# Router logits from un-normalised rows, a five-bit search for two experts, weight tiles split ahead of the first gather

## The chip, the cores and the metric

One NeuronCore of a Trainium2 chip. The time is the device time of one execution, in microseconds (us); lower is better. The kernel before: median 2549.72 us of 3 runs (2549.34 to 2553.43). Engines are named as in the profile: PE (matrix products), ACT, DVE, POOL, SP (issues transfers). Each is a queue that runs its instructions in order.

## The reference

Two layers over 1024 latent rows and 256 context rows of 1024 features. Each layer mixes the rows (Fourier heads, pooling groups, attention), projects them out, and then sends them through 16 experts, of which each takes the 128 latent rows (32 context rows) that like it best:

```python
x_new = x + g1 * ox                                   # x_mid
h = modulate(x_new, norm2_g[i], sh2, sc2)             # rms norm * g * (1 + scale) + shift
logits = jnp.einsum('bnd,de->bne', h, w_router)
aff = jax.nn.softmax(logits, axis=-1)
g, idx = lax.top_k(aff.transpose(0, 2, 1), cap)       # cap = 2 n / 16
xs = jax.vmap(lambda hb, ib: hb[ib])(h, idx)
a, u = xs @ w_gate, xs @ w_up
y = (silu(a) * u) @ w_down * g                        # scattered back and added
```

The second layer has no experts over context rows. All in float32.

## The kernel before, in words

Every value that enters a product is split into two parts (`split`, line 247: ACT copies the high part, DVE subtracts to get the low part), and each product is made of three: 6 matmuls of 128x512 for a weight tile of 128x1024. Tiles live in 43 pages of 128x1024 (`pg`), halves (`hf`) and quarters (`qt`), with 8 PSUM banks. All instructions go through one helper, so that the profile puts them all on line 107; they are told apart by tile names. A scheduler orders the instructions of each engine when the kernel is built; what sets the order is the dependences, the order in which the code emits work, and manual dependences (`tc.add_manual_dep`).

`out_proj` (line 991) goes over the row tiles (eight of the latent rows): `project(t)` (999) multiplies, adds to the residual (x_mid, `mid`), squares on ACT, takes the inverse root on POOL, and on DVE makes the modulated norm in two passes, which goes to a table in DRAM (`table`). `route(t)` (1031), one tile later, transposes the normed tile by 8 PE transposes (through `cs`, the identity), copies it on ACT (`hf`), multiplies by the router's weights in four column groups, copies (`qt`), transposes, and reduces to 16 logits per row. After the last tile come the softmax and the affinities (`aff`).

`Choice` (1081) finds, per expert, the threshold that leaves just 128 rows: `search(which)` (1107) builds the bits of the threshold three at a time in ten rounds, 7 candidates an expert. A round is: compare all affinities with all candidates (DVE), count with a product by ones (PE, 8 matmuls), keep the candidates that hold (DVE), take the maximum (DVE), set the next candidates (DVE). `finish` (1138) turns the thresholds into places. The latent rows have three groups: experts 0 to 3, 4 to 9, 10 to 15. `pick` (1174) makes a one-hot of an expert's places (DVE), multiplies it by the rows' numbers and gates (PE), and gives an index; `gather` (1211) fetches the 128 rows by an indirect transfer that POOL issues.

`Experts` (1232): `fetch` (pick and gather), `enter` (transposes and splits the gathered rows), `product` (1262: a weight tile a step: split it, 6 matmuls), `middle`, `leave` (scales and scatters to `out_dram`, by POOL), `ahead` (prefetches weight tiles into free pages). In layer 1 the first search runs alone (line 1567); then the 24 product steps of each expert (gate, up, down) run interleaved with the other two searches, a search step every two product steps. The gathers of experts 2 and 3 come right after expert 0's up product, since both belong to the first group. In layer 0 expert 0's gate and up run beside both searches of the context rows, then 8 steps of the second latent search run alone, and the rest goes beside the gate products of experts 1 to 7, seven steps each.

## Time and profile before

| | |
|---|---|
| median of 3 runs | 2549.72 us (2549.34 to 2553.43) |
| span of the profiled execution | 2549.8 us |
| PE busy | 2425.8 us, 95% |
| DVE busy | 1934.4 us, 76% |
| ACT busy | 1383.9 us, 54% |
| POOL busy | 327.6 us, 13% |
| transfers | 575.51 MB, 226 GB/s over the span |

No other time of the profiled execution than its span is given. The profile shows one execution. Its page gives busy times and 40 slices of the span; windows give the same for chosen stretches, with the granted clock of PE (1.00 is 2.4 GHz); the timeline gives single instructions, with the idle time before one and what ended it.

### The profile page before, as it was taken

The page shows a single profiled execution, that of the slowest core. Times are in us where ns is not written, and L with a number is a line of the kernel's source. Part 1 is how long each engine was busy: PE and PEld are TensorE (multiplying, and loading weights), DVE is VectorE, ACT ScalarE, POOL GpSimd, SP SyncE. Part 2 cuts the span into 40 slices and gives each one's busy share as a digit, 9 for nine tenths or more (in the row PEclk, how much of TensorE's full clock was granted, in tenths as well). Part 3 has the DMA queues.
Part 4 walks back from the last instruction along what each step waited for, and adds up shares of the span by engine and source line. Part 5 has one row for each costly group of instructions (what it writes and reads, how often), then busy time and mean ns, then how long its engine had stood idle before and what let it go on. Part 6 is the DMA issues. An engine that isn't in the chain of part 4 may idle for free. (4 is left out here: it accounts for less than half of the span.)

```text
span 2549.8 us, 39656 instructions
## 1 busy us (share of the span) xinstructions
PE 2425.8 (95%) x14709; PEld 1841.9 (72%) x14709; DVE 1934.4 (76%) x3114; ACT 1383.9 (54%) x1934; POOL 327.6 (13%) x350
## 2 busy tenths in 40 slices
PE   7999899999899999999999889899995999999998
PEld 3878667775677777777777567688774777888886
DVE  4537757756988787777777685877746999999997
ACT  4124546422555656666666412466523777787775
POOL 1321000001111011121010252100000111001100
PEclk9999999999999999999999999999996999999999
DMA  7103341547798899899897661100566999999993
GB/s 287 51 24 119 108 133 36 182 147 263 269 287 295 279 285 300 288 290 303 284 294 241 218 215 50 40 1 1 198 224 221 352 344 366 385 381 386 384 397 98
DMA packets 175074, 575.51 MB, mean 226 GB/s; under 512 B 22360, under 2 KB 35064, under 8 KB 174880
## 3 DMA queue, kind: packets, MB, share of 16 engines
q1 hardware_dynamic: 162784, 535.22, 59.1%
q0 software_dynamic: 12096, 37.75, 6.2%
q8 instruction: 115, 1.88, 0.3%
q14 instruction: 79, 0.65, 0.1%
HBM read 535.10 MB, written 37.80 MB: 225 GB/s over the span
## 5 line engine op out<-in xcount | busy, mean ns | idle before, releaser
L107 PE MATMUL banks<-pg,pg 128*128 128x512 f32 (+2 forms) x9656 | 1987.1, 393 | 10.5 <-DVE pg L107 7.8
L107 PEld LDWEIGHTS banks<-pg,pg 128*128 128x128 f32 (+1 forms) x9656 | 1451.7, 172 | 389.3 <-issue 30.2
L107 ACT ACTIVATE pg<-pg 128x1024 fp32r<-128x1024 f32 (+3 forms) x945 | 932.3, 1008 | 529.4 <-PE banks L107 348.2
L107 DVE TENSOR_TENSOR pg<-pg,pg 128x1024 fp32r<-128x1024 f32 (+3 forms) x918 | 1040.2, 1158 | 195.2 <-ACT pg L107 180.7
L107 ACT ACTIVATE pg<-banks 128x512 fp32r<-128x512 f32 (+3 forms) x438 | 243.6, 581 | 281.4 <-PE banks L107 271.6
L107 DVE TENSOR_TENSOR pg<-banks,pg 128x512 fp32r<-128x512 f32 (+2 forms) x404 | 257.4, 663 | 79.2 <-ACT pg L107 73.9
L107 PE MATMUL banks<-cs,pg 128*128 128x128 f32 x1616 | 239.3, 279 | 38.7 <-DVE pg L107 28.9
L107 PEld LDWEIGHTS banks<-cs,pg 128*128 128x128 f32 x1616 | 191.9, 142 | 93.8 <-DVE pg L107 44.2
L107 ACT ACTIVATE hf<-banks 128x512 f32<-128x512 f32 (+3 forms) x126 | 66.3, 541 | 241.5 <-PE banks L107 225.3
L107 PE MATMUL banks<-pg,hf 128*128 128x512 f32 (+1 forms) x660 | 162.7, 366 | 11.9 <-ACT pg L107 7.6
L107 PEld LDWEIGHTS banks<-pg,hf 128*128 128x128 f32 x660 | 113.2, 194 | 44.1 <-ACT pg L107 10.5
L107 DVE TENSOR_REDUCE mx<-banks 128x1 f32<-128x256 f32 (+1 forms) x136 | 106.6, 795 | 31.5 <-PE banks L107 30.5
L107 ACT ACTIVATE pg<-banks,nb 128x256 f32<-128x256 f32 (+1 forms) x136 | 104.0, 773 | 40.2 <-DVE nb L107 35.3
L107 POOL TENSOR_SCALAR rnv<-ss 128x1 f32<-128x1 f32 x38 | 17.1, 451 | 670.1 <-ACT pg L107 600.2
L107 POOL DMA_INDIRECT pg<-xtab,idxx x32 | 44.8, 1401 | 424.5 <-PE banks L107 165.9
L107 POOL DMA_INDIRECT xmid<-pg,idxx x16 | 37.3, 2329 | 446.9 <-DVE pg L107 446.9
L107 DVE TENSOR_TENSOR hf<-banks,pg 128x512 f32<-128x512 f32 x36 | 24.8, 689 | 65.6 <-PE banks L107 65.5
L107 POOL DMA_INDIRECT out_dram<-pg,idxx x16 | 36.3, 2271 | 244.6 <-DVE pg L107 116.6
L107 PE MATMUL banks<-pg,qt 128*32 128x256 f32 x1024 | 60.1, 388 | 0.5 <-ACT qt L107 0.5
L107 PE MATMUL banks<-pg,cond 128*32 128x512 f32 x256 | 56.6, 617 | 2.1 <-DMA pg<-in_ada_w_dram 2.1
L107 DVE TENSOR_TENSOR pg<-pg,hf 128x512 f32<-128x512 f32 (+1 forms) x68 | 42.5, 626 | 20.1 <-POOL hf L107 19.1
L107 PEld LDWEIGHTS banks<-pg,qt 128*32 128x32 f32 x1024 | 32.1, 112 | 26.6 <-issue 4.5
(148 smaller groups left out, 1082.9 us busy)
## 6 DMA issues: line engine op xcount, KB each, us to landing
pg<-in_w_gate_dram SPq DMA_DIRECT2D x256, 512.0 KB
pg<-in_w_up_dram SPq DMA_DIRECT2D x256, 512.0 KB
pg<-in_w_down_dram SPq DMA_DIRECT2D x256, 512.0 KB
pg<-in_ada_w_dram SPq DMA_DIRECT2D x96, 512.0 KB
pg<-in_w_in_dram SPq DMA_DIRECT2D x32, 512.0 KB
pg<-in_x_dram SPq DMA_DIRECT2D x16, 512.0 KB
pg<-in_w_out_dram SPq DMA_DIRECT2D x16, 512.0 KB
xtab<-pg SPq DMA_DIRECT2D x16, 512.0 KB
```

The costliest lines, as they stand in the source:

```text
L107: r = fn(*a, **k)
```

## The change

1. *Router.* `route` transposes x_mid instead of the normed tile. The router's weights are multiplied once by g (1 + scale) of their feature, and a bias (shift times weights) is made by eight matmuls; each tile's logits then take one more DVE operation, logit * r + bias. The norm itself moves behind the square for all tiles but the last, and behind the last logits for the last one.
2. *Search.* Four groups of latent experts: 0 and 1, 2 to 5, 6 to 10, 11 to 15. The first is searched five bits at a time: six rounds of 31 candidates an expert.
3. *Places.* Expert 1's one-hot may not come ahead of expert 0's index on DVE.
4. *Split ahead.* `begin(4)`: four weight tiles of expert 0 are split ahead of the products, in layer 1.
5. *Order of layer 1.* The second search (experts 2 to 5) runs beside the first 26 product steps, the gather of expert 2 comes at step 5 of expert 0's down product, that of expert 3 with expert 1's up product; the other two searches follow at a step every two product steps. Eight pages more are left free ahead of the first search (`spare + 8`).
6. *Order of layer 0.* Beside expert 0's products run one search of the context rows and the second latent one; the eight steps that ran alone are gone; the other three searches go beside experts 1 to 7, nine steps each.

The core of the diff:

```diff
@@ out_rows
+        SP.dma_start(cb[0:8, 0:128], part(4))
+        SP.dma_start(cb[8:16, 0:128], part(3))
+        SP.dma_start(cb[16:24, 0:128], norm2_g[i].rearrange("(k p) -> k p", p=128))
+        ps = bank()
+        PE.transpose(ps[:, 0:24], cb[0:24, 0:128], ident[:24, :24])
+        col = sm("rcol", [128, 24])
+        DVE.tensor_copy(col, ps[:, 0:24])
...
+        for k in range(KT):
+            PE.matmul(ps[:, 0:16], col[:, 8 + k:9 + k].to_broadcast([128, 128]), wr[:, k, 0:16],
+                      start=(k == 0), stop=(k == KT - 1))
+        base = sm("rbase", [128, 16])
+        DVE.tensor_copy(base, ps[:, 0:16])
...
+        DVE.tensor_tensor(out=wr, in0=wr, in1=col[:, 0:8, None].to_broadcast([128, 8, 32]), op=OP.mult)
@@ project
-            r = rsq("rn", ss, 1, D)
-            for cols in [slice(512 * n, 512 * n + 512) for n in range(2)] if t == st.nt - 1 else [slice(0, 1024)]:
-                DVE.scalar_tensor_tensor(h[:, cols], xt[:, cols], r, a2[:, cols], op0=OP.mult, op1=OP.mult)
-                DVE.tensor_add(h[:, cols], h[:, cols], b2[:, cols])
-            drop(xt)
-            SP.dma_start(table[rws, :], h.ap)
-            held[t] = h
+            held[t] = xt, h, rsq("rn", ss, 1, D)
+            if t < st.nt - 1:
+                normed(t)
+
+        def normed(t):
+            xt, h, r = held[t]
+            DVE.scalar_tensor_tensor(h.ap, xt.ap, r, a2.ap, op0=OP.mult, op1=OP.mult)
+            DVE.tensor_add(h.ap, h.ap, b2.ap)
+            SP.dma_start(table[128 * t:128 * t + 128, :], h.ap)
+            drop(h)
@@ route
-            h = held.pop(t)
+            h, _, r = held[t]
...
+            DVE.scalar_tensor_tensor(logit[:, t, :], logit[:, t, :], r, base, op0=OP.mult, op1=OP.add)
+            if t == st.nt - 1:
+                normed(t)
@@ Choice
-            self.groups = ((0, 4), (4, 6), (10, 6)) if st.nt == 8 else ((0, 8), (8, 8))
+            self.groups = ((0, 2), (2, 4), (6, 5), (11, 5)) if st.nt == 8 else ((0, 8), (8, 8))
...
-            for it in range(10):
+            J, rounds, j0 = (32, 6, 80) if n == 2 else (8, 10, 0)
+            m = J - 1
...
+            for it in range(rounds):
@@ pick
+            if e == 1:
+                tc.add_manual_dep(one.ins, picked[nm], order, reason="the first expert's place first")
@@ Experts
+        def begin(self, n):
+
+            for k in range(n):
+                raw = self.came.pop((0, "g", k))
+                wp = self.ready[0, "g", k] = Pair(page)
+                split(wp(0, 1024), raw.ap)
+                drop(raw)
@@ layers
-            ex.ahead(pre[1], spare)
+            ex.ahead(pre[1], spare + 8)
             run(cho.search(0))
...
             ex.fetch(0)
+            ex.begin(4)
             ex.fetch(1)
...
-            rest = chain(cho.search(1), cho.search(2))
+            rest = chain(cho.search(2), cch.search(1), cho.search(3))
...
-                    side = [(some(rest, 7), 7)] if e < 8 else []
+                    side = [(some(rest, 9), 9)] if e < 8 else []
...
-                    interleave((chain(ex.gate(e, True), ex.up(e, True)), 16), (cch.search(0), 20), (cch.search(1), 20))
+                    interleave((chain(ex.gate(e, True), ex.up(e, True)), 16), (cch.search(0), 20), (cho.search(1), 20))
...
-                    run(some(rest, 8))
...
-                        if 1 < e and e + 2 < NE:
+                        if e and e + 2 < NE:
                             ex.fetch(e + 2)
...
-                        if e == 0:
-                            ex.fetch(2)
-                            ex.fetch(3)
...
-                        yield from ex.down(e, False)
+                        yield from at(ex.down(e, False), {} if e else {5: lambda: ex.fetch(2)})
                         ex.leave(e)
-            interleave((products(), 24 * NE), (later(rest, 4), 12 * NE))
+            work = products()
+            interleave((some(work, 26), 26), (later(cho.search(1), 3), 24))
+            interleave((work, 24 * NE - 26), (rest, 12 * NE - 16))
```

What it does to the order of the instructions is seen at three places. First, DVE at the last row tile of layer 1, before (`hf<-banks` is half of the output projection times its gate, `pg_17221` x_mid, `pg_17278` the norm, `lmxx` the softmax's maximum):

```order
L107 TENSOR_TENSOR hf_17274<-banks,pg_16520 128x512
L107 TENSOR_TENSOR pg_17221<-pg_17221,hf_17274 128x512
L107 COPY qt_17307<-banks 128x128
L107 TENSOR_REDUCE logitx_3898<-banks 128x16
L107 SCALAR_TENSOR_TENSOR pg_17278<-pg_17221,rnr_100,pg_16522 128x512 x2
L107 TENSOR_TENSOR pg_17278<-pg_17278,pg_16527 128x512 x2
L107 COPY qt_17331<-banks 128x128
L107 TENSOR_REDUCE logitx_3898<-banks 128x16
L107 TENSOR_REDUCE lmxx_4838<-logitx_3898 128x8
```

And DVE there now (`pg_17401` is x_mid, `pg_17458` the norm; `pg_17712`, `pg_17716` and `pg_17780` are low parts of weight tiles):

```order
L109 TENSOR_TENSOR hf_17454<-banks,pg_16677 128x512
L109 TENSOR_TENSOR pg_17712<-pg_17067,pg_17711 128x1024
L109 TENSOR_TENSOR pg_17401<-pg_17401,hf_17454 128x512
L109 COPY qt_17482<-banks 128x128
L109 TENSOR_TENSOR pg_17716<-pg_17069,pg_17715 128x1024
L109 TENSOR_REDUCE logitx_3919<-banks 128x16
L109 TENSOR_TENSOR pg_17780<-pg_17071,pg_17779 128x1024
L109 SCALAR_TENSOR_TENSOR logitx_3919<-logitx_3919,rnr_101,rbase_3912 128x16
L109 COPY qt_17507<-banks 128x128
L109 SCALAR_TENSOR_TENSOR pg_17458<-pg_17401,rnr_100,pg_16679 128x1024
L109 TENSOR_REDUCE logitx_3919<-banks 128x16
L109 TENSOR_TENSOR pg_17458<-pg_17458,pg_16684 128x1024
```

Three splits of weight tiles now stand among the operations of the last tile, the first of them ahead of the last addition to x_mid, and the norm's two passes stand on either side of the last reduction.

Second, POOL's transfers at the start of the experts of layer 1, before (gathers of experts 0, 1, 2, 3 and the first scatter):

```order
L107 DMA pg_17589<-xtab_16532,idxx_5203 128x1024
L107 DMA pg_17605<-xtab_16532,idxx_5204 128x1024
L107 DMA pg_17844<-xtab_16532,idxx_5205 128x1024
L107 DMA pg_17860<-xtab_16532,idxx_5202 128x1024
L107 DMA out_dram<-pg_18125,idxx_5203 1024x1024
```

And now:

```order
L109 DMA pg_17701<-xtab_16706,idxx_5156 128x1024
L109 DMA pg_17733<-xtab_16706,idxx_5157 128x1024
L109 DMA out_dram<-pg_18341,idxx_5156 1024x1024
L109 DMA pg_18312<-xtab_16706,idxx_5158 128x1024
L109 DMA pg_18358<-xtab_16706,idxx_5155 128x1024
```

The gathers of experts 2 and 3 (`idxx_5158`, `idxx_5155`) have moved behind the scatter of expert 0.

Third, PE now at the place where expert 2's rows (`pg_18312`) are transposed; the products with `hf_18344` make expert 3's index, and those of expert 2's index stand right ahead of them; `hf_18327` is a compare of the third search:

```order
L109 MATMUL banks<-auxx_4890,hf_18344 128x5
L109 LDWEIGHTS ones_b
L109 MATMUL banks<-hf_18327,ones_b 128x35
...
L109 MATMUL banks<-pg_18460,pg_17937 128x512 x2
L109 MATMUL banks<-pg_18471,pg_17937 128x512 x2
L109 MATMUL banks<-pg_18471,pg_17938 128x512 x2
L109 MATMUL banks<-pg_18472,pg_17937 128x512 x2
L109 MATMUL banks<-pg_18486,pg_17937 128x512
L109 MATMUL banks<-cs,pg_18312 128x128 x8
```

The transposes stand nine matmuls of 128x512 behind a round of the search and the products that make the index; before, more than a hundred matmuls stood between.

## Rows read from the trace of the kernel before

**Rows 1.** The page: busy time, share and instructions of PE; its granted clock in 40 slices.

```profile
PE 2425.8 (95%) x14709; PEld 1841.9 (72%) x14709; DVE 1934.4 (76%) x3114; ACT 1383.9 (54%) x1934; POOL 327.6 (13%) x350
...
PEclk9999999999999999999999999999996999999999
```

**Rows 2.** Windows, layer 1: length; busy PE, PEld, DVE, ACT, POOL; PEclk; DMA; GB/s.

```profile
1920.00:1940.00 20.00, 6.63 (x89) 4.49 (x90) 11.44 (x43) 1.50 (x3) 2.77 (x5) 0.50 1.00 387
1940.00:1960.00 20.00, 7.90 (x82) 6.00 (x81) 11.11 (x35) 2.94 (x4) 2.50 (x2) 0.51 0.44 160
2040.00:2060.00 20.00, 19.37 (x114) 14.94 (x113) 19.52 (x34) 13.39 (x15) 3.33 (x2) 1.00 0.95 320
2300.00:2320.00 20.00, 20.00 (x104) 16.31 (x103) 18.59 (x20) 17.88 (x21) 3.29 (x2) 1.00 1.01 363
```

**Rows 3.** Timeline, layer 1's last tile: start, us, engine, operation, out<-in, [idle <-releaser].

```profile
1915.63 0.69 DVE L107 TENSOR_TENSOR pg<-pg,hf 128x512 f32<-128x512 f32 x1
...
1918.57 1.41 DVE L107 SCALAR_TENSOR_TENSOR pg<-pg,rnr,pg 128x512 f32<-128x512 f32 x2 [0.60 <-POOL rnr L107]
1919.90 1.29 DVE L107 TENSOR_TENSOR pg<-pg,pg 128x512 f32<-128x512 f32 x2
...
1920.74 1.94 PE L107 MATMUL banks<-cs,pg 128*128 128x128 f32 x8 [3.02 <-DVE pg L107]
...
1924.08 0.29 DVE L107 COPY qt<-banks 128x128 f32<-128x128 f32 x1 [2.89 <-PE banks L107]
...
1925.19 0.29 DVE L107 TENSOR_REDUCE lmxx<-logitx 128x8 f32<-128x128 f32 x1
```

**Rows 4.** Timeline, first search of layer 1: first compare, first product, start of the finish.

```profile
1927.07 0.39 DVE L107 TENSOR_TENSOR hf<-affx,cand 128x224 bf16<-128x224 f32 x1
...
1927.51 0.37 PE L107 MATMUL banks<-hf,ones_b 128*128 128x28 bf16 x8 [2.61 <-DVE hf L107]
...
1942.43 0.34 DVE L107 TENSOR_TENSOR hf<-affx,sel 128x32 bf16<-128x32 f32 x2
```

**Rows 5.** Timeline, places of expert 0, index, gather.

```profile
1945.06 2.36 DVE L107 TENSOR_TENSOR hf<-s1x,cs 128x1024 bf16<-128x1024 f32 x2
...
1946.34 0.38 PE L107 MATMUL banks<-auxx,hf 128*128 128x5 bf16 x8 [2.86 <-DVE hf L107]
...
1948.54 0.15 DVE L107 SCALAR_TENSOR_TENSOR idxx<-pkx 128x1 int32<-128x1 f32 x1
...
1949.49 1.55 POOL L107 DMA_INDIRECT pg<-xtab,idxx  x1 [19.33 <-DVE pkx L107]
```

**Rows 6.** Timeline, experts 0 and 1 of layer 1, DVE and PE.

```profile
1963.10 11.45 DVE L107 TENSOR_TENSOR pg<-pg,pg 128x1024 fp32r<-128x1024 f32 x10
...
1987.37 0.50 DVE L107 TENSOR_TENSOR hf<-affx,cand 128x336 bf16<-128x336 f32 x1
...
1988.53 0.37 PE L107 MATMUL banks<-hf,ones_b 128*128 128x42 bf16 x8
1988.75 3.59 PE L107 MATMUL banks<-pg,pg 128*128 128x512 f32 x14
```

**Rows 7.** All waits of PE from 1956 to 2130: total us, times, longest.

```profile
PE banks L107 <- DVE pg L107: 3.3, 5, 0.8
```

**Rows 8.** Timeline of POOL, scatters of experts 0 and 1 in layer 1.

```profile
2009.42 4.01 POOL L107 DMA_INDIRECT out_dram<-pg,idxx  x1 [22.43 <-DVE cand L107]
2047.75 1.56 POOL L107 DMA_INDIRECT out_dram<-pg,idxx  x1 [34.32 <-DVE pkx L107]
```

**Rows 9.** DMA issues at 1945, 1980 and 2085: gathers, times, median us to landing.

```profile
pg<-xtab,idxx POOLq DMA_INDIRECT x2, 5.0
...
pg<-xtab,idxx POOLq DMA_INDIRECT x2, 9.4
...
pg<-xtab,idxx POOLq DMA_INDIRECT x1, 11.3
```

**Rows 10.** Window of layer 0, expert 0. Columns as in rows 2.

```profile
660.00:680.00 20.00, 14.52 (x94) 10.46 (x93) 17.93 (x64) 6.32 (x8) 2.03 (x2) 0.83 0.59 190
```

77 lines of the change are left out of this document (46 added, 31 removed).

## The prediction

> **What bounds the kernel now.** I read the page first, then the windows, the timeline around the one thin place, the waits and the DMA issues. On the page [rows 1] PE is busy 2425.8 of 2549.8 us, and its clock row holds one slice of 40 that falls to 6. The windows [rows 2] show what that slice is: from 1920 to 1940 PE is busy 6.63 of 20 us at a granted clock of 0.50 (the lower level, 1.2 GHz), between the output projection of layer 1 and its first expert. Everything there is one chain: the last tile's router logits [rows 3], ten search rounds for experts 0 to 3 [rows 4], the places of expert 0, its gather, and its transposes [rows 5]. Work taken off that chain is time, one for one. After it the expert stage of layer 1 is held by two engines at once: 19.37 us of PE and 19.52 us of DVE in 20 while searches run beside the products, 20.00 and 18.59 when they are over [rows 2]. So an added search round costs there at least its slot on PE, and DVE has little room.
>
> The profiled execution (2549.8 us) is 0.1 us above the median of the runs, so the sum applies to either.
>
> **The chain to the first gather.** Router: the last transposes start at 1920.74, after both halves of the norm; x_mid is there at 1915.63 + 0.69 = 1916.32 [rows 3]. From x_mid itself they could start 4.4 us sooner. But in the new DVE order one split of a weight tile (1.14 us, ten in 11.45 [rows 6]) stands ahead of the last x_mid add, so 3.3 us sooner, at 1917.5. The copy of the logits came 3.34 us after the transposes (1924.08), so now at 1920.8. Behind it stand the norm's two passes, 1.41 + 1.29 us [rows 3], ahead of the last logits: 1920.8 + 0.29 + 1.41 + 0.23 + 1.29 + 0.2 = 1924.2 for the maximum, against 1925.19. I take **-1.0 us**; ends 0 (another split comes late) and -3.3 (the norm slips behind).
>
> Search: ten rounds took 15.36 us, from 1927.07 to 1942.43 [rows 4], less 0.50 for a compare of another search among them: 1.49 a round. A new round compares 496 elements instead of 224. The rows give 0.39 us for 224 and 0.50 for 336 [rows 4, 6], 0.001 us an element, so 0.66. The product with ones over 62 columns instead of 28 isn't shown: at least the 0.37 us of the 28 columns [rows 4], at most 0.82 (by columns). Three small operations grow by about 0.03 each. So 1.85 to 2.3 us, and I take 2.0, nearer the low end, since the eight products of 28 and of 42 columns both read 0.37 [rows 4, 6]. Six rounds are 12.0, and one compare of another search (0.39) stays among them: **-3.0 us** (-1.2 to -3.9).
>
> Places: two one-hots of 2.36 us stood ahead of the first index, which came at 1948.54; one is enough, since the product with it starts at 1946.34, 1.28 us in [rows 5]. With 0.38 for the product, a copy and the index after it, the index is there at about 1947.0: **-1.5 us**. Together the first gather starts 5.5 us sooner.
>
> **The expert stage of layer 1.** It now holds 30 rounds and three finishes instead of 20 and two. A round's slot on PE is 1988.75 - 1988.53 = 0.22 us [rows 6]; a finish has a few more and smaller products, which I put at three slots, 0.6. So +2.2 + 0.6 = **+2.8 us** on PE. On DVE the added work is larger, about 0.7 us a round, 7 us in all. Against it stand five weight tiles split before the gather lands and a sixth during it, 1.14 each, 6.8 us. PE waited for DVE 3.3 us in this stage [rows 7], and DVE can regain that when PE is held up (next paragraph). I take **-3.0**; ends 0 and -3.3. Splitting ahead gains nothing more at the first products, as far as I can see, since PE runs them at 0.51 of its clock until about 1960 [rows 2].
>
> The new wait: the gather of expert 2. Before, the gathers of experts 2 and 3 were issued together near 1984 [rows 9], and the only waits that PE has in this stage are on DVE [rows 7]. Now its index follows the second search, and the order of PE has its transposes only two eights of small products, one round and nine matmuls behind the products that make the index. After those products DVE still does the other one-hot (1.22 us), a copy, a compare and the index, some 2.2 us. From index to gather issue took 0.8 us (1948.54 + 0.15 to 1949.49 [rows 5]). Landing took 5.0 us with an idle memory system, 9.4 and 11.3 with weights streaming [rows 9]. At the new place weights stream (DMA share 0.95 in the window at 2040 [rows 2]), so I take 9.4: 12.4 us from the products on. PE has in the same time 1.3 us to the other one-hot's end, its products, the round, and nine matmuls of 0.24 us, 4.6 us in all. The stall is **+7.8 us**; ends 3.4 (a landing in 5.0) and 9.7 (in 11.3). What is queued behind: every product of PE; DVE comes three tiles further and then waits for expert 1's up product, which PE has behind the transposes. That is where the 3.0 us above is regained. POOL has the scatter of expert 0 ahead of this gather; it should be issued by then.
>
> The Trainium skill (DMA: Bandwidth & Descriptors, "Anatomy of one DMA — SWDGE (gpsimd) path") fits one such transfer as 2.0 us plus its bytes over 436 GB/s; for 512 KB an estimate from that page is 3.2 us. By that rule the stall would be 1.6 us and the sum 6.2 us lower. The rows above differ from it even where nothing else moves.
>
> **The rest.** The bias of the router is made three times by a transpose and eight matmuls of 16 columns, plus three small loads. No row shows these; the nearest, eight products of 28 columns, is 0.37 us, the other end 1.94 (eight transposes at the lower clock [rows 3]). I take 0.4 each, **+1.2** (0 to 5). The fused multiply-add per tile's logits (0.2 us) and the longer table of bits cost nothing: they lie beside PE's products in the output projection, where DVE's last halves waited for PE; without that cover they would be 0.2 us for each of 18 tiles. Two weight tiles fewer are fetched ahead of the search; PE's waits show none on weights [rows 7], so nothing.
>
> Layer 0: its expert 0 runs one search of the context and one of the latent rows beside its products, and four rounds that stood alone behind it go. PE is busy 14.52 us of 20 between 660 and 680 [rows 10], 5.5 idle. I take 3.0 of it back (0 to 5.5). Ten more rounds and a finish beside later products, where PE is full, cost 2.8. So **-0.2** (-4 to +4).
>
> **Sum.** -1.0 - 3.0 - 1.5 + 2.8 - 3.0 + 7.8 + 1.2 - 0.2 = +3.1 us: 2552.8 us. The measurement tells 0.2% (5.1 us) from no change, so this is no change.
>
> **Rivals.**
> 1. *The gather of expert 2 lands quickly.* For it: 5.0 us at the first gather, and the page's rule. Against: 9.4 at the same stage with the same stream. The stall is 3.4, the sum -1.3, 2548.4 us; with the rule's 3.2 us it would be 2546.6.
> 2. *Slower: the gather waits behind the scatter of expert 0 on POOL.* The scatters take 1.56 to 4.01 us to issue [rows 8], and the one ahead of the gather was the 4.01. If it starts less than 4 us ahead of the index, the gather starts up to 4 us later, and the stall is 11.8: 2556.8 us. Decided where the stall passes 9.8 us, since all else sums to -4.7. Against: expert 0's down product ends some 8 us of PE ahead of the index's products.
> 3. *The chain hardly shortens:* splits and norm ahead of the logits eat the router's gain, and a five-bit round takes 2.3 us. -2.7 instead of -5.5: 2555.6 us.
> 4. *Faster: everything that hides work does.* Norm behind the logits (-3.3), layer 0 at -4, the stall at 3.4: 2549.8 - 3.3 - 3.0 - 1.5 + 2.8 - 3.3 + 3.4 + 1.2 - 4 = 2542.1 us.
>
> **How the numbers follow.** The forecast has 0.43, rival 1 0.25, rival 2 0.14, rival 3 0.07, rival 4 0.11. Faster by over 0.2% (below 2544.6) takes rival 4 and some of rival 1 where layer 0 gains too: 0.26. Slower (above 2554.8) takes rivals 2 and 3 and the upper edge of the forecast: 0.30. The range reaches from near rival 4 to the forecast with a stall of 9.7 and layer 0 at +4, 2543 to 2560.
>
> **What would show it.** Right: first gather about 5.5 us earlier; six rounds near 2.0 us; a wait of PE on the gather of expert 2 near 2030 of some 8 us; almost no wait of PE on DVE around it. Wrong: no such wait, or rounds over 2.4 us, or a scatter that ends just ahead of that gather.

## The result, and the profile after

The changed kernel takes 2568.85 us (median of 4 runs, 2568.56 to 2570.76) against 2549.53 for the kernel before on the same chip (4 runs): a ratio of 1.0074, interval 1.0062 to 1.0087. It is slower by 19 us. The forecast was 2552.8 with a range up to 2560; the result lies outside.

The page after, busy time and granted clock:

```profile
span 2566.8 us, 40140 instructions
PE 2439.2 (95%) x14902; PEld 1852.2 (72%) x14902; DVE 1946.4 (76%) x3208; ACT 1384.0 (54%) x1934; POOL 333.1 (13%) x350
...
PEclk9999999999899999999999999999997999999999
```

Beside [rows 1] PE is busy 13.4 us longer. The slice of layer 1 that read 6 in the clock row reads 7, and a second one below 9 has come up: the eleventh, at some 640 to 705 us, in layer 0.

**Where the time went.** The products of the weight tiles (`banks<-pg,pg`, 128x512) come 9656 times in both kernels. I took the start of the n-th of them in each trace, counted from 0, and subtracted the one of before. A step from one column to the next is time lost or won between those two products:

```
product       1000  1600  1800  2000  3300  3700  6900  7000  7300  7400  7600  last
changed       -1.6   0.4   5.0   6.5   6.8   9.9  12.1  14.4  14.3   9.4  17.4  17.4
```

Product 1000 to 1600 is the end of attention and the output projections of layer 0, 1600 to 2000 its expert 0, 3300 to 3700 its experts 6 and 7, 6900 to 7000 the start of the output projection of layer 1, 7300 to 7400 the chain to the first gather of layer 1, and 7400 to 7600 the two experts behind it. So the chain wins 4.9 us, the stage behind it loses 8.0, and 14.3 have been lost before the chain starts. Such a row is one execution. e14 below runs the changed kernel again: its steps differ from these by up to 1.3 us, and the one from 7400 to 7600 by 3.4 (11.3 instead of 8.0).

**The chain to the first gather of layer 1** went nearly as the prediction had it. Timeline after, DVE's own (start, us, engine, line, operation, out<-in, [idle before <-releaser]):

```profile
1929.60 0.69 DVE L109 TENSOR_TENSOR hf<-banks,pg 128x512 f32<-128x512 f32 x1
1930.20 1.22 DVE L109 TENSOR_TENSOR pg<-pg,pg 128x1024 fp32r<-128x1024 f32 x1
1931.33 0.69 DVE L109 TENSOR_TENSOR pg<-pg,hf 128x512 f32<-128x512 f32 x1
...
1935.33 1.28 DVE L109 SCALAR_TENSOR_TENSOR pg<-pg,rnr,pg 128x1024 f32<-128x1024 f32 x1 [0.21 <-POOL rnr L109]
...
1938.06 0.29 DVE L109 TENSOR_REDUCE lmxx<-logitx 128x8 f32<-128x128 f32 x1
...
1939.93 0.67 DVE L109 TENSOR_TENSOR hf<-affx,cand 128x496 bf16<-128x496 f32 x1
...
1952.49 0.26 DVE L109 TENSOR_TENSOR hf<-affx,sel 128x16 bf16<-128x16 f32 x2
...
1954.96 1.23 DVE L109 TENSOR_TENSOR hf<-s1x,cs 128x1024 bf16<-128x1024 f32 x1
...
1956.86 0.16 DVE L109 SCALAR_TENSOR_TENSOR idxx<-pkx 128x1 int32<-128x1 f32 x1
```

And PE's and POOL's:

```profile
1940.66 0.57 PE L109 MATMUL banks<-hf,ones_b 128*128 128x62 bf16 x8 [5.01 <-DVE hf L109]
1942.77 0.57 PE L109 MATMUL banks<-hf,ones_b 128*128 128x62 bf16 x8 [1.53 <-DVE hf L109]
...
1957.82 1.36 POOL L109 DMA_INDIRECT pg<-xtab,idxx  x1 [14.17 <-DVE pkx L109]
...
1962.37 1.97 PE L109 MATMUL banks<-cs,pg 128*128 128x128 f32 x8 [3.71 <-DMA pg<-xtab,idxx]
```

Before, the last half started here:

```profile
1914.90 0.69 DVE L107 TENSOR_TENSOR hf<-banks,pg 128x512 f32<-128x512 f32 x1 [4.12 <-PE banks L107]
```

The split of a weight tile stands ahead of the last x_mid add, one pass of the norm ahead of the last logits, as foretold. From the last half of the projection to the maximum of the logits it is 1938.06 - 1929.60 = 8.46 us; before, from 1914.90 to the maximum at 1925.19 [rows 3], 10.29 us. A round takes 2.11 us (1942.77 - 1940.66), the compare 0.67. First compare to finish: 12.56 us against 15.36 [rows 4]. One-hot to index: 1.90 against 3.48 [rows 5]. Last half to gather: 28.22 against 34.59, so 6.4 us gained.

**Behind it,** PE at the transposes of expert 2:

```profile
2026.74 0.35 PE L109 MATMUL banks<-auxx,hf 128*128 128x5 bf16 x8
...
2029.22 3.91 PE L109 MATMUL banks<-pg,pg 128*128 128x512 f32 x9 [1.12 <-DVE pg L109]
2033.96 1.09 PE L109 MATMUL banks<-cs,pg 128*128 128x128 f32 x8 [0.83 <-DMA pg<-xtab,idxx]
...
2043.12 3.27 PE L109 MATMUL banks<-pg,pg 128*128 128x512 f32 x13 [0.86 <-DVE pg L109]
```

POOL there, then the transfers issued from 2027 to 2034 (median us to landing):

```profile
2020.26 2.51 POOL L109 DMA_INDIRECT out_dram<-pg,idxx  x1 [59.49 <-DVE cand L109]
2028.50 1.53 POOL L109 DMA_INDIRECT pg<-xtab,idxx  x1 [5.73 <-DVE pkx L109]
```

```profile
pg<-xtab,idxx POOLq DMA_INDIRECT x2, 5.8
```

The gather is issued 1.76 us after the products (the scatter is long out of the way) and lands in 5.8 us (the median of the two), not 9.4. PE waits for it 0.83 us, not 7.8. It waits for DVE before and behind, and the nine matmuls between take 3.91 us, where the prediction had 0.24 for each: in the window from 2028 to 2034 the granted clock is 0.72.

```profile
2020.00:2028.00 8.00, 7.71 (x61) 5.96 (x59) 8.00 (x25) 5.10 (x6) 2.51 (x1) 1.00 0.99 289
2028.00:2034.00 6.00, 4.04 (x14) 2.62 (x10) 5.54 (x12) 3.17 (x3) 2.65 (x2) 0.72 0.84 273
```

(Length; busy PE, PEld, DVE, ACT, POOL; clock; DMA; GB/s.) DVE has no idle time in the eight us ahead of the stop: in this execution it is DVE that is late, not the gather.

The second execution of the same kernel (e14) shows the same stop and another wait:

```profile
2026.60 2.45 PE L109 MATMUL banks<-pg,pg 128*128 128x512 f32 x9 [1.12 <-DVE pg L109]
2033.41 1.97 PE L109 MATMUL banks<-cs,pg 128*128 128x128 f32 x8 [4.37 <-DMA pg<-xtab,idxx]
```

Here the nine matmuls take 2.45 us, the two gathers land in 7.7 us (median), and PE waits 4.37 us for the first of them. Seven traces have this order of layer 1 (changed, e1, e3, e4, e6, e13, e14). PE waits for the gather 0.45 to 1.09 us in five of them, 2.74 in e4 and 4.37 in e14; from product 7400 to 7600 the five lose 7.7 to 8.2 us, e4 10.9 and e14 11.3. So most of the loss comes without the gather, and a late landing adds to it.

Where the changed kernel's 8.0 us go: PE stands 3.0 us longer (2.2 for DVE, 0.8 for the gather), the 200 weight products take 2.3 longer, the search's products 1.5, and transposes and index products that lie in the stretch the rest.

**Layer 0, expert 0.** Windows after, same columns:

```profile
640.00:660.00 20.00, 19.90 (x119) 15.22 (x118) 19.82 (x49) 12.59 (x14) 0.00 (x0) 1.00 0.98 389
660.00:680.00 20.00, 10.84 (x109) 8.16 (x109) 17.83 (x84) 3.24 (x4) 1.04 (x1) 0.66 0.27 79
680.00:700.00 20.00, 16.92 (x165) 10.68 (x164) 11.33 (x13) 9.52 (x11) 3.91 (x1) 0.83 0.71 226
```

PE is busy 10.84 us of the 20 where it had been 14.52 [rows 10]. The timeline of PE shows why:

```profile
667.20 0.25 PE L109 MATMUL banks<-hf,ones_b 128*128 128x56 bf16 x2 [1.57 <-DVE hf L109]
...
668.81 0.25 PE L109 MATMUL banks<-hf,ones_b 128*128 128x56 bf16 x2 [0.71 <-DVE hf L109]
...
685.82 1.94 PE L109 MATMUL banks<-cs,pg 128*128 128x128 f32 x8 [3.08 <-DMA pg<-ctab,idxc]
```

The products of expert 0 are over at 660, and rounds of both searches (56 columns the context's, 28 the latent rows') are left over. They run alone, a pair in 1.61 us (668.81 - 667.20), until 672. Why so many are left is in DVE's order. Its timeline beside the products, after:

```profile
647.01 0.27 DVE L109 TENSOR_TENSOR hf<-affc,cand 128x112 bf16<-128x112 f32 x1
647.20 0.38 DVE L109 TENSOR_TENSOR hf<-affx,cand 128x224 bf16<-128x224 f32 x1
647.50 1.22 DVE L109 TENSOR_TENSOR pg<-pg,pg 128x1024 fp32r<-128x1024 f32 x1
...
649.10 1.22 DVE L109 TENSOR_TENSOR pg<-pg,pg 128x1024 fp32r<-128x1024 f32 x1
...
650.46 1.22 DVE L109 TENSOR_TENSOR pg<-pg,pg 128x1024 fp32r<-128x1024 f32 x1
651.60 0.27 DVE L109 TENSOR_TENSOR hf<-affc,cand 128x112 bf16<-128x112 f32 x1
```

And before, at the same place:

```profile
644.86 0.45 DVE L107 TENSOR_TENSOR hf<-affc,cand 128x112 bf16<-128x112 f32 x2
645.24 1.22 DVE L107 TENSOR_TENSOR pg<-pg,pg 128x1024 fp32r<-128x1024 f32 x1
...
647.13 0.46 DVE L107 TENSOR_TENSOR hf<-affc,cand 128x112 bf16<-128x112 f32 x2
```

Before, a pair of rounds has one split of a weight tile in it and takes 2.3 us (647.13 - 644.86). After, it has three and takes 4.6 (651.60 - 647.01). The splits hurry on: product 1744, at the end of expert 0's gate and up products, starts at 657.5 against 661.1 before. PE gains 3.6 us there, and then waits for the rounds that stayed behind: product 1752, the first of what follows, starts at 675.1 against 670.0. The context's places and its gather come behind the rounds too (POOL issues it at 678.74; before, at 670.01), and PE waits 3.08 us for its landing, 1.57 before (2.53 in e14).

What PE waited for in that window before isn't what the prediction took it for:

```profile
667.18 0.19 PE L107 MATMUL banks<-auxc,hf 128*128 128x5 bf16 x1 [1.28 <-DVE hf L107]
...
674.24 0.37 PE L107 MATMUL banks<-hf,ones_b 128*128 128x42 bf16 x8
...
677.42 0.63 PE L107 MATMUL banks<-cs,pg 128*128 128x128 f32 x4 [1.57 <-DMA pg<-ctab,idxc]
```

Of the 5.5 us idle between 660 and 680 [rows 10], 3.9 are waits for DVE, for splits and one-hots above all, and 1.57 the wait for the context's gather. The four rounds that the code runs alone start at 674.24, 679.51, 683.50 and 686.63, with other products between them, and PE has no idle time ahead of any. Taking them away had none of this idle time to give back.

**The bias of the router,** PE in layer 1:

```profile
1809.84 1.86 PE L109 MATMUL banks<-qt,rcol 128*128 128x16 f32 x16
```

The eight products are 16 entries in the trace, and take 1.86 us of PE at the full clock (1.00 from 1800 to 1820), in a stretch where PE is busy 19.94 of 20 us. The prediction had 0.4 for each of the three sets.

### The profile page after: what moved, and what is told of

The parts are those of the page before. It is cut to its first block, busy times and chain, and to the rows that moved or that the text cites. A ratio compares the mean times of both kernels' runs of the same rounds, so it can differ in the third digit from the quotient of the medians.

```text
span 2566.8 us, 40140 instructions
## 1 busy us (share of the span) xinstructions
PE 2439.2 (95%) x14902; PEld 1852.2 (72%) x14902; DVE 1946.4 (76%) x3208; ACT 1384.0 (54%) x1934; POOL 333.1 (13%) x350
## 5 line engine op out<-in xcount | busy, mean ns | idle before, releaser
L109 DVE TENSOR_TENSOR pg<-pg,pg 128x1024 fp32r<-128x1024 f32 (+2 forms) x915 | 1041.5, 1161 | 204.1 <-ACT pg L109 185.3
L109 PEld LDWEIGHTS banks<-pg,hf 128*128 128x128 f32 x660 | 112.6, 194 | 45.2 <-ACT pg L109 10.9
L109 PEld LDWEIGHTS <-ones_b 128*128 128x128 bf16 x800 | 29.5, 99 | 48.2 <-issue 47.8
L109 PE MATMUL banks<-hf,ones_b 128*128 128x35 bf16 (+11 forms) x800 | 39.4, 182 | 23.4 <-DVE hf L109 22.6
```

The costliest lines, as they stand in the source:

```text
L109: r = fn(*a, **k)
```

## The experiments

Each ran beside the kernel before on its chip; a ratio is to that, with its interval. In the text, "changed" is the kernel after. Executions of one kernel spread by some 5 us to either side of the median (once by 11), so differences below about 2 us are left alone unless many runs stand behind them. A trace is one execution: those of e1, e3, e5, e8 and e15 lie 2.5 to 4.6 us below their medians, those of e2, e6 and e9 2.9 to 3.8 above, so that a time read from traces and one from medians need not agree. None leaves out part of the outputs' computation; the one that computes something beyond them says so.

### e1: layer 0 as it was

```diff
 class Choice:
-    self.groups = ((0, 2), (2, 4), (6, 5), (11, 5)) if st.nt == 8 else ((0, 8), (8, 8))
+    new = ((0, 4), (4, 6), (10, 6)) if old else ((0, 2), (2, 4), (6, 5), (11, 5))
...
-            rest = chain(cho.search(2), cch.search(1), cho.search(3))
+            rest = chain(cho.search(1), cho.search(2))
...
-                    side = [(some(rest, 9), 9)] if e < 8 else []
+                    side = [(some(rest, 7), 7)] if e < 8 else []
...
-                    interleave(..., (cch.search(0), 20), (cho.search(1), 20))
+                    interleave(..., (cch.search(0), 20), (cch.search(1), 20))
...
+                    run(some(rest, 8))
```

> The changed kernel with layer 0 as it was: the latent groups 0-3, 4-9, 10-15, the old interleaving with both context searches beside expert 0 and four rounds alone behind them. Layer 1 and the router stay changed. Theory A (the loss is mostly in layer 0's search order): in the traces the products of layer 0 fall back by 8.0 us at expert 0 and 3.3 us at experts 6 and 7, and both should go: about 2557.5 us (2555 to 2560). Theory B (the loss in layer 0 comes with the changed router and its extra work, wherever the searches stand): within 3 us of 2568.9.

Measured: 2562.99 us (2558.44 to 2567.95, 4 runs), ratio 1.0059 (1.0036 to 1.0081). The median is 6 us below the changed kernel, with wide scatter. Its trace, beside the changed one, is free of the steps at products 1600 to 2000 and 3300 to 3700 (9 us of the table above). So the new searches of layer 0 cost several us; how much, e13 measures better.

### e2: the second search of layer 1 earlier, so that expert 2's gather is covered

```diff
-            interleave((some(work, 26), 26), (later(cho.search(1), 3), 24))
-            interleave((work, 24 * NE - 26), (rest, 12 * NE - 16))
+            interleave((some(work, 16), 16), (cho.search(1), 21))
+            interleave((work, 24 * NE - 16), (rest, 12 * NE - 16))
```

(and the call of `ex.fetch(2)` at the second step of expert 1's gate)

> The changed kernel with the second search of layer 1 beside the first 16 product steps instead of 26, and the gather of expert 2 at step 1 of expert 1's gate. By the order of PE its transposes then stand 19.8 us of products behind the products of its index, instead of 2.8. Theory A (PE waits for that gather): the fall-back of 6.8 us between the products 7500 and 7600 goes, about 2562 us (2560.5 to 2564). Theory B (DVE is the bound of the stage, and ten rounds in 16 steps instead of 26 cost on DVE what the wait cost on PE): 2567 to 2572.

Measured: 2570.3 us (2562.7 to 2574.06, 4 runs), 1.0072 (1.005 to 1.0094). Nothing gained. PE's waits from 1955 to 2060:

```profile
PE banks L109 <- DVE hf L109: 8.7, 5, 2.8
PE banks L109 <- DMA pg<-xtab,idxx: 3.8, 1, 3.8
PE banks L109 <- DVE pg L109: 3.2, 3, 1.3
```

The wait for expert 2's gather is gone (the 3.8 is the first gather, which the chain ends in); in the changed kernel the same stretch shows 4.7 us for `hf` (compares and one-hots), 4.5 for gathers and 3.5 for splits (`pg`). The 8.7 are not what came in its place: this trace's chain lies 4.2 us later, and 6.75 of the 8.7 us (4.43 of the 4.7) are waits of the chain itself. Behind the chain one is left, at the end of the second search:

```profile
2005.36 0.32 PE L109 MATMUL banks<-hf,ones_b 128*128 128x4 bf16 x7 [1.91 <-DVE hf L109]
```

From product 7400 to 7600 this trace loses 9.4 us, against 8.0 and 11.3 in the two of the changed kernel. So the wait on the gather is not what the stage loses most of; PE waits for DVE here too, 1.91 us for the search and 1.32 and 1.02 for splits.

### e3: the bias with one product instead of eight

```diff
-        for k in range(KT):
-            PE.matmul(ps[:, 0:16], col[:, 8 + k:9 + k].to_broadcast([128, 128]), wr[:, k, 0:16],
-                      start=(k == 0), stop=(k == KT - 1))
+        DVE.tensor_tensor(out=pr, in0=wr, in1=col[:, 8:16, None].to_broadcast([128, 8, 32]), op=OP.mult)
...
+        DVE.tensor_reduce(base, pb.rearrange("p (k e) -> p e k", k=8)[:, 0:16, :], axis=AX.X, op=OP.add)
+        PE.matmul(ps[:, 0:16], cs[:, 430:431].to_broadcast([128, 128]), base, start=True, stop=True)
+        DVE.tensor_scalar(base, ps[:, 0:16], 256.0, None, op0=OP.mult)
```

> The changed kernel with the router's bias made by a multiplication and a sum on DVE and one product by a constant row, instead of eight products of 16 columns with a broadcast stationary side. Theory A (the eight products take 1.86 us on a full PE, as the trace of the changed kernel has them in layer 1): 1.6 us for each of the two that lie on a full PE, about 2565.5 us (2563.5 to 2567.5). Theory B (PE has gaps there that take it up): 2568 to 2570.

Measured: 2559.55 us (2556.73 to 2564.62, 5 runs), 1.0045 (1.003 to 1.006): 9.3 us below the changed kernel (8.7 when each is taken against before), and more than the 5.6 us that PE spends on the three sets (3 x 1.86). The traces lie 12.1 us apart, 2.2 of them ahead of product 1000, where no set stands. By the table at the end, 4.4 us come where the two sets of layer 0 stand (products 1000 to 1600), another 3.6 at expert 0 behind them (2.1 beside e14), and none at the set of layer 1, where the step stays: +2.0 with the one product, +2.3 with eight. There it is the set as a whole that costs, and e10, which makes it early, has +0.5. The first set shows in every trace: from product 1000 to 1200 the eight kernels with eight products lose 1.4 to 2.7 us, the seven with one product -0.3 to +0.2. At the second, part of the gain isn't PE's own time: near product 1600 the changed kernel waits 2.3 us for a transfer (`in_ada_w`; 1.5 in e14), e3 0.9, and before not at all.

### e4: in layer 0, the context's search before the latent rows'

```diff
-                    interleave((chain(ex.gate(e, True), ex.up(e, True)), 16), (cch.search(0), 20), (cho.search(1), 20))
+                    interleave((chain(ex.gate(e, True), ex.up(e, True)), 16),
+                               (chain(cch.search(0), call(lambda: ex.c_fetch(0)), cho.search(1)), 42))
```

> The changed kernel with one change in layer 0: beside expert 0's products the context rows' search runs first, then its gather is issued, and then the second latent search, instead of the two searches side by side. The same rounds, the same products. Theory A (the loss at expert 0 is a matter of order: the context gather's index comes 8.6 us late, since its search goes round for round with the longer latent one): the context gather is issued before 665, PE doesn't wait for it, and 5 to 9 us come back: about 2562 us. Theory B (the loss is DVE's: it has too much to do beside expert 0, whatever the order): the end of the searches stays near 672 and PE waits there for the latent one instead, 2566 to 2571.

Measured: 2572.68 us (2570.62 to 2575.43, 4 runs), 1.0092 (1.0075 to 1.0109): worse than the changed kernel. The gather of the context goes out at 672.54, six us sooner, but nine rounds of the latent search are then left alone, at 1.52 us each, until 683:

```profile
660.00:680.00 20.00, 4.28 (x72) 3.07 (x72) 15.87 (x68) 0.00 (x0) 1.04 (x1) 0.60 0.16 53
```

PE is busy 4.28 of 20 us. So it isn't the order of the two searches that costs; it is that nine latent rounds come to stand alone, without products beside them.

### e5, e7: the router's part by itself

e5 is the kernel before with the change in the router (logits from x_mid, bias by eight products, the norm's last tile around the logits). e7 is e5 with the cheap bias of e3 and the order of the first two places:

```diff
+            if e == 1:
+                tc.add_manual_dep(one.ins, picked[nm], order, reason="the first expert's place first")
```

> The kernel before with the router part alone: logits from x_mid, the bias by eight products, the norm behind; searches, groups, places, split and prefetch as before in both layers. Theory A (the chain to the first gather of layer 1 shortens by 2 to 3 us, and two of the three bias sets take 2 us each on a full PE): 2549 to 2553 us, level with before. Theory B (the router part itself holds most of the loss): over 2556. Theory C (it is a clear gain that the searches spoil): under 2547.

> The router part with the bias by one product, the searches of before in both layers, and expert 1's one-hot held behind expert 0's index; no split ahead. Theory A (router 2 to 3 us and places 1.5 us shorter on the chain, 1 us for each bias set on a full PE): 2545 to 2548 us, faster than before. Theory B (a shorter chain is taken back by a slower start of the experts, since DVE bounds it): 2549 to 2551.

Measured: e5 2558.66 us (6 runs), 1.0035 (1.0023 to 1.0047); e7 2551.17 us (11 runs), 1.0011 (1.0001 to 1.0021). In e5 the maximum of the logits comes 7.03 us after the last half of the projection, 3.3 us sooner than before, and yet the kernel loses 9 us. With the cheap bias it is within 0.2% of before.

The order of the places brought nothing here. In e7:

```profile
1942.43 2.36 DVE L109 TENSOR_TENSOR hf<-s1x,cs 128x1024 bf16<-128x1024 f32 x2
...
1945.91 0.15 DVE L109 SCALAR_TENSOR_TENSOR idxx<-pkx 128x1 int32<-128x1 f32 x1
```

A third one-hot starts at 1944.78, and the index comes 3.48 us after the first, as before [rows 5]. The same is so in e5, which lacks the order, and in e8, e10, e11 and e15, which have it (3.48 or 3.49). With four experts in the first group, expert 1's one-hot is held back and those of the others stand in its place; in each trace with the group of two it is 1.89 or 1.90.

### e6, e8: the new search of layer 1, and the split ahead

e8 is e7 with the four tiles split ahead; e6 is e1 with the cheap bias, so e8 with the search of the first two experts in layer 1.

```diff
-            ex.ahead(pre[1], spare)
+            ex.ahead(pre[1], spare + 8)
+            ex.begin(4)
```

> The changed kernel with layer 0's searches as before and the bias by one product; the new searches and the split ahead stay in layer 1. Theory A (what is left is layer 1: the chain 5 us shorter, then the wait of 7 us on the gather of expert 2 and 1 to 2 us of added rounds): 2550 to 2554 us. Theory B (layer 1's new order gains as it stands, and the whole loss was layer 0 and the bias): under 2547.

> The kernel of e7 with the four weight tiles split ahead of the first gather. Theory A (the splits stand ahead of the last x_mid addition on DVE and gain nothing later, since PE runs its first products at the lower clock): 0 to 1.5 us over e7. Theory B (DVE is relieved at the start of the experts, where it bounds): 2 to 4 us under e7.

Measured: e6 2555.97 us (11 runs), 1.0025 (1.0016 to 1.0034); e8 2551.91 us (11 runs), 1.0008 (0.9997 to 1.0019). Between e7 and e8, 0.7 us: the split ahead is worth nothing that shows. Between e8 and e6, 4.1 us: the five-bit search with its stage behind it is a loss of that size.

### e9: before, with the bias sets added and unused

The kernel before makes the three bias sets with their loads, transposes and products; nothing uses the result, so the outputs' computation is that of before.

```diff
+        PE.transpose(ps[:, 0:24], cb[0:24, 0:128], ident[:24, :24])
...
+        for k in range(KT):
+            PE.matmul(ps[:, 0:16], col[:, 8 + k:9 + k].to_broadcast([128, 128]), wr[:, k, 0:16],
+                      start=(k == 0), stop=(k == KT - 1))
+        base = sm("rbase", [128, 16])
+        DVE.tensor_copy(base, ps[:, 0:16])
```

> The kernel before, with the three bias sets of the change (three small loads, a transpose, eight products of 16 columns, two copies each) added and their result not used; nothing else. Theory A (a set costs what it holds on a full PE, some 2 us, and more where DVE's queue stands behind its copies): 5 to 8 us over before, 2555 to 2558. Theory B (the sets lie beside other work and cost 1.2 us in all, as the prediction had it): 2550 to 2552.

Measured: 2560.64 us (2557.6 to 2564.45, 6 runs), 1.0036 (1.0023 to 1.0049): 10 us. PE's records of them, grouped by form (busy us, mean ns; each overlaps the next):

```profile
L107 PE MATMUL banks<-qt,rcol 128*128 128x16 f32 x48 | 5.6, 256 | 0.0
```

48 records for 24 products. Against before, by the count of weight products: +2.7 from 1000 to 1200 (first set), +2.3 from 1500 to 1600 (second), +2.1 from 6900 to 7000 (third): 7.1 us where the sets stand. Most of the rest comes at 5600 to 6900 (+3.2), where no product of the edit stands; the other traces shift there by -2.4 to +2.7 us, so this can't be put down to the sets. The execution in this trace is 4 us above the median.

### e10, e11: with the old searches, other places for work

e10 is e8 with the last tile's norm behind the first compare and the bias of layer 1 made early. e11 is e10 without the early bias, and with the second of the context's searches moved from expert 0 of layer 0 to experts 1 to 7.

```diff
-            if t == st.nt - 1:
-                normed(t)
...
+                if self.st.name in pending:
+                    pending.pop(self.st.name)(cmp)
```

```diff
-            rest = chain(cho.search(1), cho.search(2))
+            rest = chain(cho.search(1), cch.search(1), cho.search(2))
...
-                    interleave(..., (cch.search(0), 20), (cch.search(1), 20))
+                    interleave(..., (cch.search(0), 20))
```

> The kernel of e8 (old searches, bias by one product, split ahead), with the last tile's norm placed on DVE behind the first compare of the search instead of ahead of the last logits, and layer 1's bias set made before the attention's last part. Theory A (the two norm passes hold the chain by 2.5 us, and the bias set of layer 1 costs 2.7 us where PE is full): 2546 to 2548 us, below before. Theory B (a microsecond off the chain comes back as a longer wait at the first weight tiles): 2550 to 2552.

> The kernel of e8 with the norm behind the first compare, and in layer 0 the second context search moved from beside expert 0's products to experts 1 to 7 (nine steps each, as in the change); the latent searches of layer 0 stay old. Theory A (DVE is full beside expert 0, and one search fewer lets the context gather start earlier): the context gather 4 us or more ahead of e8's, 2 to 5 us under e8. Theory B (what leaves expert 0 costs the same beside experts 1 to 7, where PE is full): within 2 us of e8, less the 2 us of the norm.

Measured: e10 2550.96 us (12 runs), 1.0006 (0.9996 to 1.0017); e11 2555.95 us (11 runs), 1.0021 (1.0012 to 1.003). In e10 the logits' maximum comes after 6.53 us, 3.8 sooner than before, and the first gather 32.68 us after the last half, 1.9 sooner; the time is that of before. In e11, with one search less beside expert 0, the gather of the context starts at 671.47, later than in e8 (664.37): an idea of mine that missed.

### e12: the new search of layer 1, with expert 2's gather well covered

```diff
-            interleave((some(work, 26), 26), (later(cho.search(1), 3), 24))
-            interleave((work, 24 * NE - 26), (rest, 12 * NE - 16))
+            interleave((some(work, 20), 20), (cho.search(1), 21))
+            interleave((work, 24 * NE - 20), (rest, 12 * NE - 16))
```

(with expert 2's rows fetched at the sixth step of expert 1's gate and transposed at the eighth step of its up product, three later than in the changed kernel; the rest, layer 0 too, as e10)

> Layer 1's new search (two experts, five bits) with everything else from e10: layer 0 as before, bias by one product and early, norm behind the first compare. The second search lies beside the first 20 product steps, and by the order of PE the transposes of expert 2 stand 16.5 us of products behind its index's products. Theory A (the wait on that gather was the whole cost of the new search in layer 1, and 20 steps leave DVE room): 2 to 4 us under e10. Theory B (DVE can't hold ten rounds in 20 steps and PE waits for compares instead, as in e2): 1 to 5 us over e10.

Measured: 2553.55 us (12 runs), 1.0008 (0.9999 to 1.0016), 2.6 above e10 and, by the interval, not to be told from before. The first gather starts 27.78 us after the last half, 6.8 sooner than before. PE's waits from 1950 to 2060:

```profile
PE banks L109 <- DMA pg<-xtab,idxx: 3.8, 1, 3.8
PE banks L109 <- DVE pg L109: 3.0, 5, 0.9
PE banks L109 <- DVE hf L109: 0.8, 1, 0.8
```

The 3.8 is again the first gather; there is no other wait on a transfer. Still, of 5.4 us that e12 wins at the chain (products 7300 to 7400) it has given back 6.6 by product 7600. With no stall on a gather behind the chain, the shorter chain is paid for in the two experts that follow: PE waits 2.5 us (for DVE, but for 0.3), the search's products take 1.6 more than before, the weight products 1.3, and the rest are transposes and index products that lie in the stretch.

### e13, e14: the new groups of layer 0 in the old place, and the changed kernel again

```diff
-            rest = chain(cho.search(2), cch.search(1), cho.search(3))
+            rest = chain(cho.search(1), cho.search(2), cho.search(3))
...
-                    interleave(..., (cch.search(0), 20), (cho.search(1), 20))
+                    interleave(..., (cch.search(0), 20), (cch.search(1), 20))
+                    run(some(rest, 8))
```

(the rest of that search goes beside expert 1's gate, 13 steps where there were 9, with the gather of expert 2 behind it; the searches beside experts 2 to 7 take 7 steps each)

> The changed kernel, layer 0 alone changed back in the place of its searches: both context searches beside expert 0 and four rounds alone behind them as before, but with the new groups; the rest of the second latent search (experts 2 to 5) beside expert 1's gate, the gathers of experts 2 and 3 behind that. Theory A (expert 0's stretch is lost because the latent search took the place of the cheaper second context search, so that the first context search ends late): the 8 us between the products 1600 and 2000 go, the rounds beside experts 1 to 7 stay: 2562 to 2565 us. Theory B (the new groups themselves, an added search of ten rounds, cost it wherever they stand): 2567 to 2571.

> The changed kernel once more, beside the others of this call: 2567 to 2571 us if its earlier four runs stand; the sum of the parts measured alone (bias sets 10, layer 0's searches 4 to 10, layer 1's search 3 to 4, less 2 to 3 for the chain) would give 2565 to 2571.

Measured: e13 2561.02 us (2558.44 to 2562.01, 5 runs), 1.0039 (1.0025 to 1.0052); e14, the changed kernel, 2569.6 us (2567.88 to 2570.9, 5 runs), 1.0073 (1.0059 to 1.0086). 8.6 us apart, without overlap. The window of e13:

```profile
660.00:680.00 20.00, 17.02 (x95) 11.97 (x93) 18.07 (x60) 8.64 (x10) 1.38 (x1) 0.83 0.50 162
```

PE is busy 17.02 us, against 10.84 in the changed kernel, and 4 rounds alone cover the context's gather again. Between products 1600 and 2000 nothing is lost (the table's 6.1, 4.6 in e14, is 0.0 here); the step at 3300 to 3700 stays (+2.7, after +3.1), so that belongs to the ten more rounds, and the rest to the place of the search.

### e15: before, with the places' order and the split ahead

> The kernel before with two parts of the change alone: expert 1's one-hot behind expert 0's index, and four weight tiles split ahead of the first gather (with eight pages more left free). Router and searches as before. Theory A (1.5 us off the chain, and the splits don't hold it): 2547 to 2549 us. Theory B (the splits among the last tile's operations on DVE take it back): 2550 to 2552.

The edits are those shown at e7 and e8, on the kernel before. Measured: 2557.26 us (2552.0 to 2560.51, 11 runs), 1.0029 (1.002 to 1.0038): 6.7 us slower. In layer 1 the splits delay the logits' maximum by 0.9 us, the places' order brings nothing (see e7), and the first gather starts 35.55 us after the last half instead of 34.59. The larger loss is in layer 0, +4.2 us between products 1600 and 1700, where the edit orders one operation and nothing else; the clock granted from 630 to 640 is 0.51, where it is 1.00 before. Beside e7 to e8, where the same splits cost nothing, this isn't settled.

The table of the n-th weight product, for the runs that decide:

```
product       1000  1600  1800  2000  3300  3700  6900  7000  7300  7400  7600  last
changed       -1.6   0.4   5.0   6.5   6.8   9.9  12.1  14.4  14.3   9.4  17.4  17.4
e3            -3.8  -6.2  -4.6  -3.7  -3.6  -0.6   0.2   2.2   2.2  -2.6   5.1   5.3
e13           -0.9  -0.1  -0.8  -0.1   0.4   3.1   3.6   5.6   5.6   1.1   9.3   9.7
e14           -2.1  -1.2   2.6   3.4   3.7   6.8  10.3  12.5  12.4   6.8  18.1  18.4
e9            -0.6   4.4   5.8   5.8   5.9   5.9  10.4  12.5  12.5  13.2  13.2  12.9
e10           -2.2  -7.5  -5.4  -5.4  -5.1  -5.4  -2.0  -1.5  -1.0  -1.8  -0.9  -0.9
e12           -2.5  -7.9  -2.7  -2.7  -2.3  -2.6   1.1   1.8   2.7  -2.7   3.9   3.3
```

## Why the prediction was wrong, point by point

The medians give a ladder, each run less the kernel before on its own chip: changed +19.3; with the cheap bias +10.6 (e3); with the old layer 0 as well +6.2 (e6); with the old search of layer 1 as well +2.2 (e8); without the split ahead +1.4 (e7). So the bias is 8.7 us, layer 0 4.4, the search of layer 1 4.0, the rest 2.2, within the spread of zero. (The order matters: with the dear bias in, the place of layer 0's search alone gives 8.6 by e13, and layer 0 as a whole 5.3 by e1, whose four runs spread over 9.5 us.)

- **"The rest: the bias ... 0.4 each, +1.2 (0 to 5)".** The step that failed most. The size is 10 us by itself (e9), 8.7 to 9.3 within the change (e3), and 7.5 between e5 and e7. Two things were wrong in it. The price: I took the eight products of 28 columns [rows 4], which share one stationary side (`ones_b`) and are bf16; these are f32 and load another side for each, 16 records at 0.12 us (which of the two makes the price no run separates). The upper end, 1.94 [rows 3], was the right one, and it is reached at the full clock. And the set as a whole: where one stands, the products behind fall back by 2.1 to 2.7 us (e9), more than the 1.86. The remaining 3 us or so lie elsewhere and are not explained.
- **"Layer 0: -0.2 (-4 to +4)".** The second step that failed, and in sign. I let 3.0 us of PE's idle time there come back because four rounds that stood alone go; but that idle time was waits for DVE and for the context's gather, and none of it stood ahead of those rounds. I took it that the ten rounds put in their place would run beside the products, and did not look at DVE's order, where three splits now cut each pair of rounds. Five pairs of rounds come to stand alone instead of four rounds, and hold back the gather of the context by 8.7 us. Lost: 6.1 us in the trace (4.6 in e14); e13 puts the search elsewhere and gets 8.6 back. The 2.8 us for ten more rounds beside later products is right: +3.1 at products 3300 to 3700.
- **The chain: -1.0, -3.0, -1.5.** Right: -1.8, -2.8, -1.6 in the trace, first gather 6.4 us sooner against 5.5. A round takes 2.11 us (2.0), the compare 0.67 (0.66), and the product with 62 columns 0.57, between the ends. The places gained by the group of two: the dependence alone (item 3 of the change) leaves them as they were (e7). Two readings were off without effect on the sum: three one-hots, not two, started ahead of the first index, and the last transposes started inside the norm's second pass (1919.90 to 1921.19 [rows 3]), not behind both halves.
- **The stage behind it: +2.8 - 3.0 + 7.8 = +7.6.** The third step that failed, in its mechanism; that the size comes near is luck. The trace has +8.0 from product 7400 to 7600 (+11.3 in e14), and another +1.6 at the end of the last search, which is given back by the end. Of the stall only 0.83 us is the gather's, which landed in 5.8 us (4.37 and 7.7 in e14); I took 9.4 from [rows 9]. Its index was also issued sooner than I had it (1.76 us after the products, not 3.0), and PE came later. The rest is DVE, late with splits and compares, weight products that run longer, and the added rounds. "DVE regains 3.0" did not happen: PE still waits for splits, 3.5 us between 1955 and 2060 (1.4 before). With the gather covered, 9.4 us (e2) and 6.6 us (e12) are lost all the same.
- **The landing of the gather.** From the fit in the Trainium skill (DMA: Bandwidth & Descriptors, "Anatomy of one DMA — SWDGE (gpsimd) path") an estimate for 512 KB is 3.2 us. The traces show more, 5.8 and 7.7 us here and 5.0 at the least, and less than the 9.4 that I took.
- **Splitting ahead: nothing.** Right on top of the cheap router (e8 against e7); e15, on the kernel before, is at odds with it and stays open.
- **The rivals.** The first (the gather lands quickly) came true as an event in five of seven traces, and the time it promised did not, since DVE filled the place. The second (behind the scatter on POOL) did not occur: the scatter starts at 2020.26, the gather at 2028.50. Nor did the third: the chain shortened by 6.4 us. The fourth assumed that whatever hides work goes on hiding it, which is what failed.

- **The signs and the range.** The first gather and the rounds came as foretold; the wait of some 8 us on the gather and the near absence of waits on DVE did not, and the first of these two was named as a sign of being wrong. The range's upper edge took the ends of the stall and of layer 0, but not the 5 us that the bias has as its own end.

No version that ran is faster than before; e8, e10 and e12 can't be told from it, and e7 is within 0.2%.

## What to carry to other kernels

Price a small matmul from a row of the same form (type, and whether each loads its own stationary side), and where no such row exists and PE is full, take the upper bound. Before a search is moved beside products, read in the order of the engine that both use how many splits now stand between two rounds: rounds that fall behind come out alone, and push back whatever waits on them. A thin chain made shorter is time won only if the work taken from it lands where PE and DVE both have room; here they had little, and 5 us won came back as 8 lost, 11 in a second execution.

## What the runs showed that I had not expected

- Eight f32 products of 16 columns show as 16 records and take 1.86 us, at the full clock; eight bf16 products of 62 columns, 0.57 us in a stretch at 0.50.
- The gather of 512 KB landed in 5.8 us while weights streamed (DMA share 0.84 in that window), in 7.7 in a second execution of the same kernel (0.94), and had taken 9.4 and 11.3 in the same stage before.
- PE stood for 1.12 us at 2028, and the nine matmuls behind took 3.91 us, with the granted clock at 0.72 of the full one (2.4 GHz) over that window. In six of the seven traces with this order they took 3.81 to 3.93 us; in e14, behind the same stop, 2.45, and the clock was 0.90 over that window. At 640 to 700 in layer 0, 1.00 fell to 0.66 in the stretch where PE did only rounds, and was 0.83 in the next.
- Between two kernels the time of a stretch that an edit doesn't touch can shift by some us (e9 at products 5600 to 6900, e15 at 1600 to 1700). Two executions of one kernel differ by up to 3.4 us in a step of the table, so part of this may be scatter; its cause is open.
